# A planner with other durations: longer 1024-element VectorE instructions, longer GpSimd and ScalarE instructions

## Chip, cores and metric

The kernel runs on one core of a Trainium2 chip, in one launch. The metric is the device time of an execution in microseconds. The core has five engines that run side by side, each with its own queue in a fixed order: TensorE (PE; its weight loads are listed apart as PEld), VectorE (DVE), ScalarE (ACT), GpSimd (POOL) and SyncE (SP), which here issues the transfers. An instruction waits on semaphores for what other engines make.

## The reference, cut to what matters

256 tokens of width 1024 in f32 go through two blocks. The first has two layers, each a mixer of four branches and a gated FFN with a short convolution; the second one layer: a two-way state-space scan and attention, then a mixture of experts with 16 experts in four groups, and a last layer norm.

```python
for l in range(DEPTH):                       # DEPTH = 2
    h = rms_norm(x, norm_mix_pre[l])
    proj = h @ w_in[l]                       # queries, keys, values, conv and pool inputs
    ...                                      # o_a: compressed, selected and window attention
    o_b = conformer_conv(b_in, ...)          # depthwise convolution of 31 taps
    o_c = pool_mixer(c_in, ...)
    o_d = banded_attention(qd, ...)          # with sinks
    up = jnp.einsum("bsnc,ncd->bsnd", branches, w_branch[l])
    gates = jax.nn.sigmoid((h @ w_gate[l]).reshape(...))
    mix = jnp.einsum("bsnd,bsnd->bsd", gates, up) @ w_o[l]
    x = x + rms_norm(mix, norm_mix_post[l])
    hf = rms_norm(x, norm_ffn_pre[l])
    u = causal_depthwise_conv(hf @ ffn_w_up[l], ...)
    gate, val = jnp.split(u, 2, axis=-1)
    x = x + rms_norm((gelu(gate) * val) @ ffn_w_down[l], norm_ffn_post[l])
...                                          # second block: scan, attention, MoE, layer norm
```

## The kernel before

**Work.** Nearly all time goes into products of the 256 tokens with weights, 290 MB of f32 that are read from HBM once, mostly in units of 128 x 1024 (512 KB, tiles `wr_wr`). TensorE multiplies a rounded f32 form, so that each unit is split in two: ScalarE copies it into the rounded high half `wh_wh`, and GpSimd or VectorE subtracts this from the unit and writes the low half `wl_wl` (function `sp`). Three products, high x high, low x high and high x low, are then added up in a PSUM bank (`ps_bank`). Activations are split in the same way into `hp_hTh` and `hp_hTl`. Which of the two engines makes a low half is decided while the kernel is written down, by a share for each kind of weight (0.92 of the FFN's go to GpSimd, 0.12 of the experts'), not by the planner.

**Around the products.** VectorE also adds up the 31 taps of the conformer convolution, one instruction for each tap and bank (`ps_bank<-wk_cpad,pp_cwh,ps_bank`), makes softmax rows, their transposed low halves and rotary sums (all `wk_t2k`), the reciprocal square roots of the norms as rows of 128x1 instructions (`wk_sm`, `wk_nw`, `wk_nwy`), normalised tokens (`wk_t4k`, `cp_x`) and the router's numbers (`wk_rt`). ScalarE reads PSUM banks out, takes Squares and exponentials.

**The order.** No instruction is issued when it is written down. The class `Rec` records every one with its engine, its operands and the instructions that it depends on. `Rec.order` then plays a list scheduler (`run`) over the record ten times (`ROUNDS`): each engine takes from its ready instructions the one with the earliest latest-start time, within a small window; PSUM banks and SBUF slots have to be free; transfers have a modelled queue, TensorE a modelled clock. Between VectorE and GpSimd `run` holds a lock: an instruction of one that reads SBUF in the manner marked `port` doesn't start before the last such instruction of the other has ended (`held`). After each round `slack` goes backward through the plan and sets the latest-start times for the next. The shortest of the ten plans is kept, and `emit` issues the instructions in its order, all from one line, which is why every row of the profile carries L540. All durations in this play come from `Rec.cost`, a formula for each engine with a fixed part and a part by elements. They set the order alone: on the chip an instruction starts when its queue and its semaphores allow.

**What the formulas said and what the trace has.** For a split of 128 x 1024, `cost` before gives ScalarE 0.109 + 1024/1200 = 0.962 us, VectorE 0.075 + 1024/920 = 1.188 us, GpSimd 0.148 + 1024/464 = 2.355 us.

## Time and profile before

| | us |
|---|---|
| median of 3 runs | 1503.31 |
| lowest to highest | 1502.95 to 1504.41 |
| the profiled execution | 1503.68 |
| its span | 1501.6 |

The span is the time from the first instruction to the last as the profiler has it; the execution's own time is 2.1 us longer. In the profile, busy time is the time in which an engine executes. A wait is time in which it stood idle before an instruction, put down to the engine and tile whose result came last. The span falls into stages: the first layer's mixer up to about 290 us, its FFN to about 500, the second layer to about 1050, the second block's projections, scan and attention to about 1290, the experts to about 1480, and the last layer norm.

### The profile page before, as it was taken

The page shows a single profiled execution, that of the slowest core. Times are in us where ns is not written, and L with a number is a line of the kernel's source. Part 1 is how long each engine was busy: PE and PEld are TensorE (multiplying, and loading weights), DVE is VectorE, ACT ScalarE, POOL GpSimd, SP SyncE. Part 2 cuts the span into 40 slices and gives each one's busy share as a digit, 9 for nine tenths or more (in the row PEclk, how much of TensorE's full clock was granted, in tenths as well). Part 3 has the DMA queues.
Part 4 walks back from the last instruction along what each step waited for, and adds up shares of the span by engine and source line. Part 5 has one row for each costly group of instructions (what it writes and reads, how often), then busy time and mean ns, then how long its engine had stood idle before and what let it go on. Part 6 is the DMA issues. An engine that isn't in the chain of part 4 may idle for free.

```text
span 1501.6 us, 23962 instructions
## 1 busy us (share of the span) xinstructions
PE 1433.5 (95%) x8276; PEld 1234.6 (82%) x8276; DVE 1035.5 (69%) x2412; ACT 980.7 (65%) x1777; POOL 976.0 (65%) x504
## 2 busy tenths in 40 slices
PE   8989999989999899999999999999999999889994
PEld 6968888879999698788888999999897778768773
DVE  5898622277665779987526733336998876789997
ACT  4876944566555577887447755556677786478772
POOL 5796499848777577947897677776666761342211
PEclk9999999999999999999999999999999999799998
DMA  8555365648888574647757555555543214359881
GB/s 308 167 171 189 114 203 181 215 138 279 281 288 273 188 253 143 207 139 238 240 167 255 162 184 189 186 184 158 169 138 107 94 50 143 127 187 327 332 288 73
DMA packets 91155, 290.35 MB, mean 193 GB/s; under 512 B 11409, under 2 KB 13713, under 8 KB 91026
## 3 DMA queue, kind: packets, MB, share of 16 engines
q1 hardware_dynamic: 91026, 288.74, 57.8%
q8 instruction: 67, 1.10, 0.3%
q14 instruction: 62, 0.51, 0.1%
HBM read 287.13 MB, written 1.05 MB: 192 GB/s over the span
## 4 chain that ended last, share of the span: by engine, by line
PE 82%; DVE 8%; ACT 4%; issue 3%; POOL 1%; DMA 1%; SPq 0%; ACTq 0%; POOLq 0%; DVEq 0%
PE ps_bank L540 82%; DVE ps_bank L540 2%; ACT wh_wh L540 1%; DVE wk_t2k L540 1%; DVE wk_t4k L540 1%; DVE wl_wl L540 1%; POOL wl_wl L540 1%; ACT wk_t2k L540 1%; ACT wk_t4k L540 1%; DVE wk_sm L540 1%; DMA wr_wr<-w_qd 1%; DVE wk_nw L540 0%; ACT hp_hTh L540 0%; ACT ps_bank L540 0%; DVE cp_x L540 0%
## 5 line engine op out<-in xcount | busy, mean ns | idle before, releaser
L540 POOL TENSOR_TENSOR wl_wl<-wr_wr,wh_wh 128x1024 fp32r<-128x1024 f32 (+2 forms) x346 | 822.2, 2386 | 431.2 <-ACT wh_wh L540 416.0
L540 ACT ACTIVATE wh_wh<-wr_wr 128x1024 fp32r<-128x1024 f32 (+2 forms) x446 | 464.0, 1045 | 307.3 <-PE ps_bank L540 185.0
L540 PE MATMUL ps_bank<-hp_hTh,wh_wh 128*128 128x256 f32 x928 | 266.1, 287 | 1.4 <-DVE hp_hTl L540 1.4
L540 PE MATMUL ps_bank<-wh_wh,hp_hTh 128*128 128x512 f32 (+3 forms) x656 | 258.0, 396 | 6.1 <-ACT hp_hTh L540 4.0
L540 PE MATMUL ps_bank<-hp_hTh,wl_wl 128*128 128x256 f32 x928 | 262.8, 283 | 0.2 <-POOL wl_wl L540 0.2
L540 PE MATMUL ps_bank<-hp_hTl,wh_wh 128*128 128x256 f32 x928 | 262.6, 283 | 0.0
L540 PE MATMUL ps_bank<-wl_wl,hp_hTh 128*128 128x512 f32 (+3 forms) x656 | 256.3, 391 | 1.0 <-DVE wl_wl L540 1.0
L540 PE MATMUL ps_bank<-wh_wh,hp_hTl 128*128 128x512 f32 (+3 forms) x656 | 254.8, 389 | 0.6 <-DVE hp_hTl L540 0.6
L540 DVE TENSOR_TENSOR wl_wl<-wr_wr,wh_wh 128x1024 fp32r<-128x1024 f32 (+2 forms) x100 | 152.8, 1543 | 72.3 <-ACT wh_wh L540 70.5
L540 PEld LDWEIGHTS ps_bank<-hp_hTh,wh_wh 128*128 128x128 f32 x928 | 177.6, 191 | 4.3 <-DVE hp_hTl L540 1.7
L540 PEld LDWEIGHTS ps_bank<-hp_hTl,wh_wh 128*128 128x128 f32 x928 | 177.7, 192 | 2.5 <-issue 1.2
L540 PEld LDWEIGHTS ps_bank<-hp_hTh,wl_wl 128*128 128x128 f32 x928 | 177.7, 191 | 0.4 <-POOL wl_wl L540 0.4
L540 PE MATMUL ps_bank<-wh_wh,wk_t4k 128*128 128x512 f32 (+2 forms) x496 | 153.6, 383 | 0.0
L540 PEld LDWEIGHTS ps_bank<-wh_wh,hp_hTh 128*128 128x128 f32 x656 | 124.5, 190 | 33.6 <-ACT hp_hTh L540 6.5
L540 DVE SCALAR_TENSOR_TENSOR wk_t2k<-ps_bank,cl_cols,wk_t2k 128x255 f32<-128x255 f32 (+1 forms) x176 | 84.5, 481 | 96.9 <-ACT wk_t2k L540 94.0
L540 PEld LDWEIGHTS ps_bank<-wl_wl,hp_hTh 128*128 128x128 f32 x656 | 125.2, 191 | 26.9 <-issue 1.9
L540 PEld LDWEIGHTS ps_bank<-wh_wh,hp_hTl 128*128 128x128 f32 x656 | 124.5, 190 | 27.2 <-DVE hp_hTl L540 2.9
L540 DVE SCALAR_TENSOR_TENSOR ps_bank<-wk_cpad,pp_cwh,ps_bank 128x256 f32<-128x256 f32 x232 | 110.2, 486 | 4.4
L540 PEld LDWEIGHTS ps_bank<-wh_wh,wk_t4k 128*128 128x128 f32 x496 | 90.9, 188 | 18.0 <-DVE wk_t4k L540 0.3
L540 ACT ACTIVATE wk_t2k<-ps_bank 128x512 fp32r<-128x512 f32 (+6 forms) x156 | 81.7, 532 | 26.1 <-PE ps_bank L540 23.7
L540 PE MATMUL ps_bank<-wl_wl,wk_t4k 128*128 128x512 f32 (+2 forms) x248 | 94.7, 382 | 0.6 <-DVE wl_wl L540 0.6
L540 ACT ACTIVATE wk_t2k<-wk_t2k,wk_sm 128x128 f32<-128x128 f32 (+2 forms) x200 | 84.8, 457 | 10.0 <-DVE wk_sm L540 9.5
(310 smaller groups left out, 2586.5 us busy)
## 6 DMA issues: line engine op xcount, KB each, us to landing
wr_wr<-w_up SPq DMA_DIRECT2D x88, 512.0 KB, 4.0
wr_wr<-w_gate SPq DMA_DIRECT2D x64, 512.0 KB, 4.2
wm_wm<-w_mod SPq DMA_DIRECT2D x96, 256.0 KB, 4.4
wr_wr<-w_down SPq DMA_DIRECT2D x44, 512.0 KB, 4.3
wr_wr<-w_gu SPq DMA_DIRECT2D x40, 512.0 KB, 5.4
wr_wr<-w_br SPq DMA_DIRECT2D x32, 512.0 KB, 4.5
wk_t4k<-w_gu SPq DMA_DIRECT2D x24, 512.0 KB, 6.6
wr_wr<-w_xbc SPq DMA_DIRECT2D x22, 512.0 KB, 4.4
```

The costliest lines, as they stand in the source:

```text
L540: getattr(getattr(r.nc, o.e), o.f)(*[real(x) for x in o.a], **{n: real(x) for n, x in o.kw.items()})
```

## The change

Three of the durations in `Rec.cost` are set to other values. ScalarE's fixed part grows from 0.066 to 0.08 with a PSUM operand and from 0.109 to 0.13 without, and it takes 1150 instead of 1200 elements a microsecond. GpSimd goes from 0.148 + n/464 to 0.25 + n/440. A VectorE instruction whose largest operand has 1024 elements for each partition, none of them in PSUM, counts 1.55 us. For the 128 x 1024 split that is 1.020 us on ScalarE, 1.55 on VectorE and 2.577 on GpSimd. VectorE's other 1024-element additions and products on SBUF data count 1.55 as well.

```diff
--- before.py
+++ after.py
@@ -255,7 +255,7 @@
         n = max(_size(x) for x in vs)
         ptr = sum(type(o.kw.get(x)) is View for x in ("bias", "scale", "accum_out"))
         if o.e == "scalar":
-            return (0.066 if vs[1].t.psum else 0.109) + n / 1200 + 0.093 * ptr, o.a[2] if len(o.a) > 2 else None
+            return (0.08 if vs[1].t.psum else 0.13) + n / 1150 + 0.093 * ptr, o.a[2] if len(o.a) > 2 else None
         if o.e == "vector":
             if o.f in ("tensor_scalar", "scalar_tensor_tensor"):
                 ptr = sum(type(x) is View and _size(x) == 1 for x in o.a[2:4]) if n > 1 or o.f == "tensor_scalar" else 0
@@ -265,10 +265,12 @@
                 n *= 6
             if o.f in ("tensor_scalar", "tensor_copy", "tensor_single_scalar") and not any(x.t.psum for x in vs):
                 n /= 2
+            if n == 1024 and not any(x.t.psum for x in vs):
+                return 1.55, None
             return 0.075 + n / 920 + 0.06 * ptr, None
         if o.f == "memset":
             return 0.035 + n / 1200, None
-        return 0.148 + n / 464, None
+        return 0.25 + n / 440, None
 
     def follow(r, o, p):
```

The record is the same: the same instructions on the same engines with the same dependencies. The plan made from it differs. 73% of TensorE's instructions keep their place in its queue, 64% of GpSimd's, 47% of ScalarE's and 29% of VectorE's, many of these last being taps of the convolution that exchange places with one another. In the FFN and gate stages the order is nearly the same. Line 540 becomes line 542. The numbers behind the names below count records and differ between the two.

VectorE in the attention of the second layer, before. `wk_sm` is the reciprocal of the softmax sums, the `wk_cpad` rows are taps, and the last two rows make low halves of transposed softmax rows, which TensorE multiplies with the values next:

```order
L540 TENSOR_TENSOR wk_t2k_6441<-wk_t2k_6426,ps_bank_6398 64x512
L540 TENSOR_TENSOR wk_sm_1_6205<-ps_bank_6418,wk_sm_1_6205 128x8
L540 RECIPROCAL wk_sm_6_6455<-wk_sm_1_6205 128x8
L540 SCALAR_TENSOR_TENSOR ps_bank_6109<-wk_cpad_1797,pp_cwh_5545,ps_bank_6109 128x256 x8
L540 TENSOR_TENSOR wk_t2k_6441<-wk_t2k_6489,ps_bank_6453 64x512
L540 SCALAR_TENSOR_TENSOR ps_bank_6109<-wk_cpad_1797,pp_cwh_5545,ps_bank_6109 128x256 x16
L540 TENSOR_TENSOR wk_t2k_6592<-ps_bank_6531,wk_t2k_6582 128x512
L540 TENSOR_TENSOR wk_t2k_6601<-ps_bank_6566,wk_t2k_6587 128x512
```

and after:

```order
L542 TENSOR_TENSOR wk_t2k_6452<-wk_t2k_6425,ps_bank_6395 64x512
L542 TENSOR_TENSOR wk_sm_1_6194<-ps_bank_6412,wk_sm_1_6194 128x8
L542 RECIPROCAL wk_sm_6_6468<-wk_sm_1_6194 128x8
L542 SCALAR_TENSOR_TENSOR ps_bank_6086<-wk_cpad_1810,pp_cwh_5533,ps_bank_6086 128x256 x15
L542 TENSOR_TENSOR wk_t2k_6452<-wk_t2k_6538,ps_bank_6438 64x512
L542 TENSOR_TENSOR wk_t2k_6556<-ps_bank_6518,wk_t2k_6548 128x512
L542 SCALAR_TENSOR_TENSOR ps_bank_6086<-wk_cpad_1810,pp_cwh_5533,ps_bank_6086 128x256 x3
L542 TENSOR_TENSOR wk_t2k_6581<-ps_bank_6554,wk_t2k_6570 128x512
L542 SCALAR_TENSOR_TENSOR ps_bank_6086<-wk_cpad_1810,pp_cwh_5533,ps_bank_6086 128x256
```

The first of the two low halves (128x512, from `ps_bank` and `wk_t2k`), behind 8 and 16 taps before, stands behind 15 taps now, and three taps stand between it and the second.

VectorE ahead of the router, before. `cp_x` is the residual stream, which is normalised here one token tile at a time; BN_AGGR ends the statistics of the second tile:

```order
L540 BN_STATS wk_sm_1_14645<-cp_x_73 128x6
L540 TENSOR_SCALAR cp_x_73<-cp_x_73,wk_sm_14603,wk_nwy_14634 128x512
L540 BN_AGGR wk_sm_14679<-wk_sm_1_14645 128x2
L540 TENSOR_SCALAR wk_nw_14684<-wk_sm_14679 128x1
L540 TENSOR_SCALAR wk_nw_14686<-wk_nw_14684 128x1
L540 TENSOR_SCALAR wk_nw_14691<-wk_nw_14686,wk_nw_14684 128x1
L540 TENSOR_SCALAR wk_nw_14695<-wk_nw_14691 128x1
L540 TENSOR_SCALAR wk_nwy_14697<-wk_nw_14695,wk_nw_14686 128x1
L540 COPY wk_t2k_14699<-ps_bank_14688 128x512
L540 TENSOR_SCALAR wk_nw_14691<-wk_nwy_14697,wk_nw_14684 128x1
```

and after:

```order
L542 BN_STATS wk_sm_1_14648<-cp_x_73 128x6
L542 BN_AGGR wk_sm_14660<-wk_sm_1_14648 128x2
L542 TENSOR_SCALAR wk_nw_14662<-wk_sm_14660 128x1
L542 TENSOR_SCALAR wk_nw_14669<-wk_nw_14662 128x1
L542 TENSOR_SCALAR wk_nw_14672<-wk_nw_14669,wk_nw_14662 128x1
L542 TENSOR_SCALAR wk_nw_14675<-wk_nw_14672 128x1
L542 TENSOR_SCALAR wk_nwy_14677<-wk_nw_14675,wk_nw_14669 128x1
L542 TENSOR_SCALAR wk_nw_14672<-wk_nwy_14677,wk_nw_14662 128x1
L542 TENSOR_SCALAR cp_x_73<-cp_x_73,wk_sm_14617,wk_nwy_14643 128x512
L542 TENSOR_SCALAR wk_nwy_14690<-wk_nw_14672,wk_nwy_14677 128x1
L542 TENSOR_SCALAR wk_sm_14693<-wk_sm_14660,wk_nwy_14690 128x1
L542 TENSOR_SCALAR cp_x_73<-cp_x_73,wk_sm_14660,wk_nwy_14690 128x512
```

The normalisation of the first tile (the first `cp_x<-cp_x,wk_sm,wk_nwy`) stood ahead of the second tile's BN_AGGR and now stands behind it, with six instructions between.

VectorE at the start of the experts, before. The CAST reads a PSUM bank out and the next adds another part:

```order
L540 TENSOR_TENSOR wl_wl_14967<-wr_wr_14562,wh_wh_14959 128x1024
L540 CAST wk_t4k_14976<-ps_bank_14880 128x512
L540 TENSOR_TENSOR wk_t4k_14987<-ps_bank_14880,wk_t4k_14976 128x512
L540 SCALAR_TENSOR_TENSOR wk_t1k_14997<-wk_t1k_14997,ps_bank_14941 128x256
L540 SCALAR_TENSOR_TENSOR wk_t1k_14997<-wk_t1k_14997,wk_ws_14922,ps_bank_14941 128x256
L540 TENSOR_TENSOR wl_wl_15027<-wr_wr_14625,wh_wh_14990 128x1024
L540 TENSOR_TENSOR wl_wl_15048<-wr_wr_14675,wh_wh_15001 128x1024
L540 TENSOR_TENSOR wl_wl_15067<-wr_wr_14649,wh_wh_15013 128x1024
L540 TENSOR_TENSOR wk_t2k_15021<-ps_bank_15017,wk_t2k_15021 128x256
L540 TENSOR_TENSOR wl_wl_15081<-wr_wr_14744,wh_wh_15025 128x1024
L540 TENSOR_TENSOR wl_wl_15085<-wk_t4k_14416,wh_wh_15046 128x1024
L540 SCALAR_TENSOR_TENSOR wk_t1k_15063<-wk_t1k_15063,ps_bank_14994 128x256
```

and after:

```order
L542 TENSOR_TENSOR wl_wl_14966<-wr_wr_14568,wh_wh_14958 128x1024
L542 TENSOR_TENSOR wl_wl_15000<-wr_wr_14601,wh_wh_14977 128x1024
L542 SCALAR_TENSOR_TENSOR wk_t1k_14992<-wk_t1k_14992,ps_bank_14946 128x256
L542 SCALAR_TENSOR_TENSOR wk_t1k_14992<-wk_t1k_14992,wk_ws_14927,ps_bank_14946 128x256
L542 TENSOR_TENSOR wl_wl_15022<-wr_wr_14638,wh_wh_15005 128x1024
L542 TENSOR_TENSOR wl_wl_15050<-wr_wr_14652,wh_wh_14995 128x1024
L542 TENSOR_TENSOR wk_t2k_15037<-ps_bank_15026,wk_t2k_15037 128x256
L542 TENSOR_TENSOR wl_wl_15065<-wr_wr_14715,wh_wh_15020 128x1024
L542 TENSOR_TENSOR wl_wl_15087<-wk_t4k_14416,wh_wh_15031 128x1024
L542 TENSOR_TENSOR wl_wl_15102<-wk_t4k_14465,wh_wh_15062 128x1024
L542 SCALAR_TENSOR_TENSOR wk_t1k_15077<-wk_t1k_15077,ps_bank_14989 128x256
L542 CAST wk_t4k_15052<-ps_bank_14883 128x512
```

The two reads of the bank, second and third before, have gone behind the first splits (the first is the last row here, the second follows two rows later), and the third and the fourth of the `wl_wl` rows have changed places.

## Rows read from the trace of the kernel before

**Rows 1.** The page, span and part 1: busy us, share, instructions.

```profile
span 1501.6 us, 23962 instructions
...
PE 1433.5 (95%) x8276; PEld 1234.6 (82%) x8276; DVE 1035.5 (69%) x2412; ACT 980.7 (65%) x1777; POOL 976.0 (65%) x504
```

**Rows 2.** TensorE's waits: releaser, us in total, times, longest.

```profile
PE ps_bank L540 <- DVE wk_t4k L540: 8.8, 6, 4.2
PE ps_bank L540 <- DVE wl_wl L540: 7.5, 7, 2.2
PE ps_bank L540 <- DVE wk_t2k L540: 4.7, 5, 1.9
...
PE ps_bank L540 <- DVE wk_nw L540: 3.7, 1, 3.7
```

**Rows 3.** The page, part 5: groups with count, busy us, mean ns, idle before.

```profile
L540 POOL TENSOR_TENSOR wl_wl<-wr_wr,wh_wh 128x1024 fp32r<-128x1024 f32 (+2 forms) x346 | 822.2, 2386 | 431.2 <-ACT wh_wh L540 416.0
...
L540 DVE TENSOR_TENSOR wl_wl<-wr_wr,wh_wh 128x1024 fp32r<-128x1024 f32 (+2 forms) x100 | 152.8, 1543 | 72.3 <-ACT wh_wh L540 70.5
...
L540 DVE SCALAR_TENSOR_TENSOR ps_bank<-wk_cpad,pp_cwh,ps_bank 128x256 f32<-128x256 f32 x232 | 110.2, 486 | 4.4
```

**Rows 4.** Timelines, MoE start: start us, duration, instruction, [idle before <-releaser].

```profile
1324.32 0.68 DVE L540 CAST wk_t4k<-ps_bank 128x512 fp32r<-128x512 f32 x1
...
1327.60 9.52 DVE L540 TENSOR_TENSOR wl_wl<-wr_wr,wh_wh 128x1024 fp32r<-128x1024 f32 x3
...
1337.38 3.07 DVE L540 TENSOR_TENSOR wl_wl<-wr_wr,wh_wh 128x1024 fp32r<-128x1024 f32 x1
1340.38 1.21 DVE L540 TENSOR_TENSOR wl_wl<-wk_t4k,wh_wh 128x1024 fp32r<-128x1024 f32 x1
...
1332.70 6.67 POOL L540 TENSOR_TENSOR wk_t4k<-wk_t4k,wk_t4k 128x1024 f32<-128x1024 f32 x2
...
1337.18 0.72 PE L540 MATMUL ps_bank<-wl_wl,wk_t2k 128*128 128x512 f32 x2 [1.88 <-DVE wl_wl L540]
```

**Rows 5.** Timelines and busy time by stretch, second layer's attention.

```profile
585.11 0.50 PE L540 MATMUL ps_bank<-wk_t2k,wk_Vd 128*128 128x512 f32 x1 [1.89 <-DVE wk_t2k L540]
...
584.36 1.29 DVE L540 TENSOR_TENSOR wk_t2k<-ps_bank,wk_t2k 128x512 fp32r<-128x512 f32 x2
...
core 0: us, PE busy (x) PEld busy (x) DVE busy (x) ACT busy (x) POOL busy (x), PEclk, DMA share, GB/s
560.00:630.00 70.00, 65.62 (x375) 54.68 (x374) 65.71 (x172) 58.41 (x130) 60.16 (x37) 1.00 0.54 176
```

**Rows 6.** Timelines of ScalarE and TensorE between the two layers.

```profile
507.06 2.01 ACT L540 ACTIVATE wh_wh<-wr_wr 128x1024 fp32r<-128x1024 f32 x2 [2.26 <-issue]
...
513.25 1.97 PE L540 MATMUL ps_bank<-cp_ident,wk_t4k 128*128 128x128 f32 x8 [4.19 <-DVE wk_t4k L540]
```

**Rows 7.** Timelines of VectorE and TensorE ahead of the router.

```profile
1293.49 1.18 DVE L540 TENSOR_SCALAR cp_x<-cp_x,wk_sm,wk_nwy 128x512 f32<-128x512 f32 x1
...
1305.27 0.18 DVE L540 TENSOR_TENSOR wk_rt<-ps_bank,c_rows 128x20 f32<-128x20 f32 x1 [2.14 <-PE ps_bank L540]
...
1306.49 0.60 PE L540 MATMUL ps_bank<-wk_rt,c_const 128*128 128x8 f32 x2 [1.26 <-DVE wk_rt L540]
```

**Rows 8.** Timelines of TensorE and VectorE near the end of the MoE.

```profile
1468.03 0.50 PE L540 MATMUL ps_bank<-wl_wl,wk_t2k 128*128 128x512 f32 x1 [2.15 <-DVE wl_wl L540]
...
1464.55 3.42 DVE L540 TENSOR_TENSOR wl_wl<-wr_wr,wh_wh 128x1024 fp32r<-128x1024 f32 x1
```

**Rows 9.** Busy time by stretch, columns as in the fifth group.

```profile
512.50:519.50 7.00, 6.07 (x19) 4.47 (x20) 6.82 (x18) 3.96 (x8) 5.98 (x4) 0.56 0.59 199
1338.50:1345.50 7.00, 6.03 (x17) 4.23 (x16) 7.00 (x7) 2.86 (x3) 0.87 (x1) 0.56 0.77 239
1352.00:1482.00 130.00, 123.42 (x539) 97.51 (x538) 125.57 (x139) 93.95 (x113) 24.80 (x9) 1.00 0.78 284
```

## The prediction, made before the changed kernel had run

> **What bounds the kernel now.** The page comes first. TensorE is busy for 1433.5 of 1501.6 us, the other three engines for about two thirds of the span [rows 1]. As the mean share mixes stages, the next view is TensorE's list of waits. Its four lines that matter here hold 24.7 us: VectorE's token sums and normalised rows (`wk_t4k`), the low halves of weights that VectorE makes (`wl_wl`), low halves of softmax rows (`wk_t2k`), and one reciprocal square root (`wk_nw`) [rows 2]. All four end on VectorE. So a new order can gain only where VectorE, or what feeds it, hands TensorE something late; where TensorE runs without a gap (the FFN and gate stages), moving other engines' work about costs and gains nothing as long as it stays ahead.
>
> The change alters no instruction, no dependency and no engine, only the durations from which the planner makes its order. Nothing can be gained by work that is gone. The sum is therefore one of waits: at each place where TensorE waits, I compare what stands ahead of the awaited instruction on its engine before and after, price what moved by its duration in the trace, and ask what is late next.
>
> **What the new durations are worth as numbers.** The VectorE split of 128x1024 takes 1543 ns as a mean over 100, the GpSimd one 2386 ns over 346 [rows 3]. But the VectorE mean is made of two kinds: 1.21 us alone, and about 3.1 us while GpSimd runs an add on SBUF data (three in 9.52 us from 1327.60 on, one of 3.07, one of 1.21; two of GpSimd's adds took 6.67 us together) [rows 4]. The planner already lets one of the two wait for the other (`held` in `run`). With 1.55 for every VectorE instruction of 1024 elements without a PSUM operand it books a part of that price twice, and where there is no GpSimd work it books too much. So the plan isn't simply a truer one; only the places tell.
>
> **The places, one by one.** Gains are positive.
>
> A, attention of the second layer, 571 to 585 us. Before, VectorE ran 24 convolution taps between the reciprocal and the `wk_t2k` subtraction that TensorE waited for; one tap has 486 ns on average over 232 [rows 3]. The subtraction, first of a pair, started at 584.36, and TensorE, idle for 1.89 us, went on at 585.11 [rows 5]. Now 15 taps stand there, and three more come between the pair. That is nine taps or 4.4 us less; four taps ahead of the reciprocal are gone as well. The subtraction's own inputs may hold it up for a part of that, but 1.89 us earlier is within reach, and the wait is gone. What it costs: VectorE may stand still before it, and it is busy for 65.71 of 70 us in this stretch [rows 5], so that the taps put off must still be run. I take 1.5, between 0 (all given back at the next such wait) and 1.9.
>
> B, the norms between the first layer's FFN and the second layer's mixer, 504 to 516 us. ScalarE ran a second weight split ahead of the Squares from which VectorE makes the rstd; two splits took 2.01 us [rows 6], one therefore 1.0. It now stands behind four Squares. TensorE's 4.19 us wait that ended at 513.25 [rows 6] hangs on this chain, but also on VectorE's row of small instructions, of which the Square is only the start. I take 0.7, between 0 and 1.0.
>
> C, layer norm ahead of the MoE router, 1291 to 1306 us. VectorE ran the 1.18 us normalisation of token tile 0 before the statistics of token tile 1 were aggregated; it now comes six small instructions later, and the chain of tile 1 gets ahead of it. The router's first `wk_rt` on tile 1 ran at 1305.27, behind 2.14 us in which VectorE waited for TensorE, and TensorE waited 1.26 us for it in turn [rows 7]. The chain of tile 1 moves up by 1.18 from this alone, and by up to 2 of VectorE's 2.14 us if ScalarE's and TensorE's part of the chain follows. Against that, a weight split of about 1.2 us now stands in front of the copy of tile 0's transposes. I take 1.2, between -0.5 and 2.0.
>
> D, the first weight splits of the MoE, 1324 to 1345 us. Before, VectorE made two reads of a PSUM bank first, from 1324.32 on [rows 4], then met GpSimd's four adds with all of its next four splits: 9.52 us for three, 3.07 for the fourth, and TensorE waited 1.88 us at 1337.18 for one of them [rows 4]. Now the first split comes before the two reads, which move ten places back, and the split that TensorE waited for comes one earlier. The adds' input on ScalarE moves four places back, behind three more splits of 1.0 us each [rows 6]; I estimate that about 2 of these 3 us reach the adds. So about one split less meets an add: one meeting costs 9.52 / 3 - 1.21 = 2.0 us. The reads, however, now fall into the full stretch behind. I take 1.5, between -2 (one meeting more, with the reads in the way) and 3.8 (the 1.88 gone, and as much again of the 7.5 us line [rows 2]).
>
> E, near the end, 1462 to 1470 us. TensorE waited 2.15 us at 1468.03 for a split that took 3.42 us, as it met a GpSimd split that began at the same moment [rows 8]. It now stands three places, some 2.3 us, earlier on VectorE. It may still meet the GpSimd split. I take 1.0, between 0 and 2.15.
>
> F, the norms ahead of the first layer's FFN at 316 us, the wait of 3.7 us for `wk_nw` [rows 2]. Here ScalarE and VectorE run one or two more instructions of the tap's size, half a microsecond each [rows 3], in front of the chain: loss 0.6, between 0 and 1.1.
>
> Elsewhere places of both signs, each under 1 us, are near a wait; I count them at nothing, plus or minus 2.
>
> Sum: 1.5 + 0.7 + 1.2 + 1.5 + 1.0 - 0.6 = 5.3 us. The profiled execution had 1503.68 us, so 1498.4; it lies 0.37 above the median of 1503.31, so the forecast against the median is **1498.0 us**. The half widths of the terms (1.0, 0.5, 1.3, 2.9, 1.1, 0.6 and 2) give about 4 us when they don't all fall to one side: 1494 to 1502 for this case alone.
>
> **A rule against it.** The rows show the meeting itself: while GpSimd adds ran, a VectorE split took 3.2 us and an add 3.3, against 1.21 us for a split alone [rows 4]. The Trainium skill (SBUF — State Buffer, section "Who interferes with whom") says of this that the two share one port pair under an exclusive lock, for the whole instruction, and that the one that comes second blocks. By that rule the price of a split is 1.2 us or that plus the rest of the other's instruction, never 1.55, and the flat figure misleads the planner wherever it has to choose who meets whom; the time by it is the second rival's, 1506.5, instead of 1498. Rows and rule agree on the waiting; which order it makes the planner choose no trace here shows.
>
> **The rivals.**
>
> R1, given back. VectorE's work in the places A, D and E is the same in sum and only exchanged; in the stretch of A it is busy for 65.71 of 70 us and from 1352 to 1482 us for 125.57 of 130, about as much as TensorE with 123.42 [rows 5, 9]. Then a wait removed comes back at the next hand-over, A, D and E are worth nothing, and B, C and F remain: 0.7 + 1.2 - 0.6 = 1.3, which gives 1502.0. For it speak those two lines; against it that TensorE's waits in them sit where VectorE's awaited instruction stood behind work that nobody was waiting for.
>
> R2, more meetings at the port. The four adds of place D and the reads slide into the stretch from 1345 on, where VectorE is full. Each further meeting costs 2.0 us there and nothing hides it. With three more, and nothing gained in D and E, it is 6.0 - (1.5 + 0.7 + 1.2 - 0.6) = 3.2 us slower: 1506.5. It decides from two more meetings on (4.0 - 2.8 = 1.2 slower); with one it is lost in the forecast. For it speaks that the new figures make the planner count a meeting less as something to avoid; against it that GpSimd has just 24.80 us of work in those 130 us [rows 9].
>
> R3, the clock. In the 7 us that follow the long wait at 513 TensorE was granted 0.56 of its clock, mostly the lower of its two levels (1.2 instead of 2.4 GHz), while busy for 6.07 us; after the wait at 1337 it is 0.56 again, with 6.03 us busy [rows 9]. If the waits of B and D shrink so far that the clock doesn't fall behind them, up to 3 us of each are gained: 5.3 + 6 gives 1492. For it speaks that the low stretches begin right after those waits; against it that B leaves 3.5 of 4.19 us standing, and that VectorE paces the other place anyway.
>
> **How the numbers follow.** The forecast gets 0.46, R1 0.26, R2 0.17, R3 0.11. The bound of what a measurement of this kernel tells from no change is 0.2%, 3 us. R3 and nearly all of the forecast lie on the faster side (0.55); R1 and the forecast's upper end are within it (0.28); R2 is slower (0.17). The range has to leave out no more than 2 in 10: it reaches from a part of R3 at 1490 up to half a microsecond beyond R2's 1506.5, as its price per meeting is open.
>
> **What the profile after would show.** TensorE's waits for `wk_t2k` lose the 1.89 us one; the wait between the layers falls from 4.19 to about 3.5; `wk_rt` runs 1 to 2 us earlier against the start of its stage; the splits at the start of the MoE show two or three durations near 3 us instead of four; the wait at 1468 is shorter than 1. Busy times of VectorE and GpSimd change only by meetings: VectorE's 1035.5 us falls by 2 to 4. It is wrong if VectorE's busy time grows by 5 or more (R2), if the waits named are gone but others of their size stand right behind them (R1), or if the granted clock's mean moves by a hundredth (R3, upwards). A new wait in a stage that I took to run without a gap, FFN or gates, would be a cause that none of these holds.

## The result and the profile after

The median after is 1520.76 us over 4 runs (1517.24 to 1525.12), that of before in the same comparison 1503.29. The ratio is 1.0117, with a 95% interval of 1.0102 to 1.0133: the kernel is 17.5 us slower. The forecast was 1498.0 with a range up to 1507, so that sign and range are both wrong. The profiled execution took 1519.78 us, with a mean granted clock of 0.978 (0.981 before).

The page of the kernel after, span and part 1, answers to [rows 1]:

```profile
span 1517.9 us, 23992 instructions
...
PE 1440.6 (95%) x8276; PEld 1237.8 (82%) x8276; DVE 1035.2 (68%) x2412; ACT 981.5 (65%) x1777; POOL 969.9 (64%) x504
```

The counts of the four engines are the same, as they must be. VectorE is busy for 1035.2 us instead of 1035.5, GpSimd for 6.1 us less. TensorE's 8276 instructions took 7.1 us longer, at a mean granted clock that is 0.003 lower; the other 9.2 of the span's 16.3 us are idle time. TensorE's waits in the kernel after (releaser, us in total, times, longest), to be set beside [rows 2]:

```profile
PE ps_bank L542 <- DVE wk_sm L542: 7.3, 5, 3.0
PE ps_bank L542 <- DVE wk_nw L542: 6.4, 2, 6.1
PE ps_bank L542 <- ACT wk_t4k L542: 6.2, 6, 2.6
PE ps_bank L542 <- DVE wk_t4k L542: 5.5, 8, 1.2
PE ps_bank L542 <- DVE wk_t2k L542: 5.4, 7, 1.7
PE ps_bank L542 <- DVE wl_wl L542: 4.9, 5, 2.1
```

Two more lines of before, for the comparison:

```profile
PE ps_bank L540 <- ACT wk_t4k L540: 2.3, 3, 1.4
PE ps_bank L540 <- DVE wk_sm L540: 2.1, 2, 1.3
```

The longest lines of before have shrunk (`wk_t4k` 8.8 to 5.5, `wl_wl` 7.5 to 4.9), as the forecast had it. Others have grown: VectorE's `wk_sm` from 2.1 to 7.3, ScalarE's `wk_t4k` from 2.3 to 6.2, `wk_nw` from 3.7 to 6.4. The groups of low halves in part 5 of the page after, against [rows 3]:

```profile
L542 POOL TENSOR_TENSOR wl_wl<-wr_wr,wh_wh 128x1024 fp32r<-128x1024 f32 (+2 forms) x346 | 818.9, 2376 | 433.6 <-ACT wh_wh L542 399.7
...
L542 DVE TENSOR_TENSOR wl_wl<-wr_wr,wh_wh 128x1024 fp32r<-128x1024 f32 (+2 forms) x100 | 147.9, 1489 | 78.7 <-ACT wh_wh L542 78.3
```

A VectorE split takes 1489 ns on average instead of 1543, so that meetings cost VectorE a little less than before, not more. Yet the idle time before VectorE's splits that ends on ScalarE has grown from 70.5 to 78.3 us.

**Where the time goes.** The engines run the same instructions, so that each TensorE instruction has a twin in before. The table sets the start of an instruction against that of its twin, takes the median over those within 4 us of a stage's edge, and gives what each stage adds (us; plus is lost; stages by the clock of before; one profiled execution of each kernel). E1 has ScalarE's new formula alone, E2 VectorE's, E3 GpSimd's; E8 changes two of ScalarE's numbers by a nanosecond; E17 has 1.55 in the experts alone; E13 is the change with the old formulas in the experts; E20 has other figures. All are told below.

| stage | change | E1 | E2 | E3 | E8 | E17 | E13 | E20 |
|---|---|---|---|---|---|---|---|---|
| 0-285, first mixer | -2.2 | -0.9 | -0.8 | +3.6 | -2.1 | -2.1 | -0.8 | -1.9 |
| 285-340, norms ahead of FFN | +3.3 | +0.1 | +0.4 | +1.9 | +0.4 | 0.0 | +3.1 | +0.7 |
| 340-500, FFN | +0.3 | +0.3 | 0.0 | +0.3 | 0.0 | 0.0 | +0.3 | +0.3 |
| 500-580 | 0.0 | -0.9 | +1.0 | -0.9 | 0.0 | +1.3 | -0.3 | +1.8 |
| 580-600 | -2.3 | -2.0 | -2.5 | -1.4 | -0.6 | +1.6 | -2.3 | -1.5 |
| 600-640, attention | +5.4 | +3.9 | +2.0 | +4.0 | +3.7 | 0.0 | +5.5 | +1.8 |
| 640-785 | +0.1 | -0.5 | +0.9 | -0.8 | -1.1 | +0.5 | +0.1 | +0.4 |
| 785-850, norms ahead of FFN | +4.3 | +3.0 | +2.1 | +10.8 | +2.2 | 0.0 | +4.0 | +2.7 |
| 850-1050, FFN | -0.4 | -0.1 | -0.1 | -0.4 | -0.1 | 0.0 | -0.4 | +0.6 |
| 1050-1235 | +2.8 | 0.0 | -0.8 | -0.4 | -0.6 | 0.0 | +2.8 | +0.6 |
| 1235-1290 | +1.4 | +1.0 | +0.5 | +0.2 | 0.0 | 0.0 | +1.4 | +4.5 |
| 1290-1325, router | -3.0 | -0.5 | +0.2 | -3.5 | -2.9 | +0.1 | -3.0 | +0.2 |
| 1325-1360, first experts | +2.8 | +0.1 | -1.6 | -0.6 | -2.0 | -0.6 | -0.6 | +0.2 |
| 1360-1430, experts | +4.8 | +0.5 | +5.0 | 0.0 | +0.6 | +5.1 | +1.7 | +0.8 |
| 1430-1483, last experts | -1.1 | -2.0 | +1.6 | -1.8 | -1.6 | +2.7 | -1.7 | -1.4 |
| at the end | +16.3 | +1.8 | +7.9 | +10.9 | -4.0 | +8.4 | +9.8 | +9.5 |

E17 also says how far such a table can be trusted: its order is that of before up to the experts, and still its first stage differs by 2.1 us and those around 500 to 600 by 1.3 and 1.6. From 600 to 1325 it keeps to before within 0.1, but for 0.5 in one stage. So the change's -2.2 in the first stage is no gain of its plan: the same order has -2.1 there.

### The profile page after: what moved, and what is told of

Same layout as the page of the kernel before. It is cut to its first block, busy times and chain, and to the rows that moved or that the text cites. A ratio compares the mean times of both kernels' runs of the same rounds, so it can differ in the third digit from the quotient of the medians.

```text
span 1517.9 us, 23992 instructions
## 1 busy us (share of the span) xinstructions
PE 1440.6 (95%) x8276; PEld 1237.8 (82%) x8276; DVE 1035.2 (68%) x2412; ACT 981.5 (65%) x1777; POOL 969.9 (64%) x504
## 4 chain that ended last, share of the span: by engine, by line
PE 66%; DVE 7%; issue 4%; ACT 2%; POOL 1%; DMA 1%; SPq 0%; ACTq 0%; DVEq 0%; POOLq 0%
PE ps_bank L542 66%; DVE ps_bank L542 2%; DVE wl_wl L542 1%; DVE wk_t4k L542 1%; DVE wk_t2k L542 1%; ACT wh_wh L542 1%; DVE wk_sm L542 1%; POOL wl_wl L542 1%; ACT wk_t2k L542 1%; DVE wk_nw L542 0%; ACT wk_t4k L542 0%; ACT ps_bank L542 0%; DMA c_cols<-cols 0%; DMA wr_wr<-w_gu 0%; ACT hp_hTh L542 0%
## 5 line engine op out<-in xcount | busy, mean ns | idle before, releaser
L542 DVE TENSOR_TENSOR wl_wl<-wr_wr,wh_wh 128x1024 fp32r<-128x1024 f32 (+2 forms) x100 | 147.9, 1489 | 78.7 <-ACT wh_wh L542 78.3
```

The lines of the kernel that those rows point to most:

```text
L542: getattr(getattr(r.nc, o.e), o.f)(*[real(x) for x in o.a], **{n: real(x) for n, x in o.kw.items()})
```

## The experiments

First the median in us, then the ratio to the kernel before, both run side by side, with its 95% interval. It is formed over all the executions and can lie 0.1 to 0.2% from the ratio of two medians; costs are added up by it.

**E1 to E4: whose figure.** Each makes one part of the change alone; the fourth adds a nanosecond to VectorE's fixed part, a difference that says nothing about the chip but makes another plan (88% of TensorE's and 46% of VectorE's instructions keep their places). Theory 2 in these expectations is scatter: any new plan of this planner costs about as much.

```diff
 E1  -            return (0.066 if vs[1].t.psum else 0.109) + n / 1200 + 0.093 * ptr, ...
 E1  +            return (0.08 if vs[1].t.psum else 0.13) + n / 1150 + 0.093 * ptr, ...
 E2  +            if n == 1024 and not any(x.t.psum for x in vs):
 E2  +                return 1.55, None
 E3  -        return 0.148 + n / 464, None
 E3  +        return 0.25 + n / 440, None
 E4  -            return 0.075 + n / 920 + 0.06 * ptr, None
 E4  +            return 0.076 + n / 920 + 0.06 * ptr, None
```

> Only ScalarE's new formula; VectorE and GpSimd as before. Theory 1 (the flat 1.55 us for VectorE does the harm, as it books the meetings with GpSimd twice): within 4 us of before, 1500 to 1507. Theory 2 (no single figure does it: any other plan loses some us against the one of before, whose order happens to fit): 1507 to 1518. Theory 3 (GpSimd's 2.577 us does it): as theory 1 here.

> Only VectorE's flat 1.55 us for 1024 elements. Theory 1: nearly the whole loss, 1515 to 1523. Theory 2: a loss of the same kind as in the other three, 1507 to 1518. Theory 3: 1500 to 1507.

> Only GpSimd's new formula. Theory 1: 1500 to 1507. Theory 2: 1507 to 1518. Theory 3: nearly the whole loss, 1515 to 1523.

> None of the three figures: VectorE's fixed part is 0.076 instead of 0.075 us, 1 ns more for each instruction, which says nothing about the hardware but gives another plan. Theories 1 and 3: within 2 us of before. Theory 2: a loss as in the other three runs, 1507 to 1518, since it is the other draw that costs and not the figure.

E1: 1503.59, ratio 0.9998 [0.9985, 1.0012]. E2: 1510.62, 1.0039 [1.0024, 1.0054]. E3: 1513.58, 1.0063 [1.0043, 1.0083]. E4: 1502.28, 0.9982 [0.9967, 0.9997]. The parts cost -0.02 + 0.39 + 0.63 = 1.00%, the whole 1.17 (1.02 to 1.33). ScalarE's figure alone is free, and a new plan alone isn't slower, so theory 2 falls as the sole cause. Theories 1 and 3, each of which put nearly the whole loss (1515 us and more) on one figure, fall too: neither E2 nor E3 gets there.

**E5 to E8: another draw.** If the losses belonged to the particular plans, a nanosecond on top would deal them anew. E5 is the whole change, E6 is E3 and E7 is E2, each with E4's nanosecond; E8 is before with a nanosecond on both of ScalarE's fixed parts. Theory A: the figures cost what they cost, whatever the draw.

```diff
 E5, E6, E7  -            return 0.075 + n / 920 + 0.06 * ptr, None
 E5, E6, E7  +            return 0.076 + n / 920 + 0.06 * ptr, None
 E8          -            return (0.066 if vs[1].t.psum else 0.109) + ...
 E8          +            return (0.067 if vs[1].t.psum else 0.110) + ...
```

> All three figures as in the change, with VectorE's fixed part at 0.076 instead of 0.075 us: another draw of the same kind. Theory A (the figures cost, whatever the draw): 1516 to 1525, like the change. Theory B (each plan is a draw, and the figures only set off another one): 5 us or more away from the change, most likely below it.

> GpSimd's new formula alone, with the same 1 ns on VectorE. Theory A: 1510 to 1517, like the run with GpSimd's formula alone. Theory B, with what the trace of that run shows (ScalarE stands 4.3 us behind a late transfer of a small table at 810 us, 8 us lost in that stretch): 1503 to 1507 if that instruction falls behind others again, 1512 if not.

> VectorE's flat 1.55 us alone, with the same 1 ns on its other instructions. Theory A: 1508 to 1514, and the loss again lies in the experts' stage from 1360 to 1460 us, where VectorE is full. Theory B: 5 us or more away from 1510.6, or the loss lies elsewhere.

> None of the three figures: ScalarE's fixed parts 1 ns longer. Theory A: within 3 us of before. Theory B: spread as wide as between the other kinds, 1500 to 1515.

E5: 1529.47, 1.0141 [1.0096, 1.0186]. E6: 1515.42, 1.0067 [1.0046, 1.0088]. E7: 1518.21, 1.0083 [1.0059, 1.0108]. E8: 1499.96, 0.9971 [0.9954, 0.9989]. The kinds stay apart in sign: in both draws each of the two figures costs 0.4 to 0.8%, and both together about the sum (0.67 + 0.83 = 1.50 in the second, 1.41 measured). But E7 costs twice as much as E2, with intervals that don't touch, and the two null plans gain 0.2 and 0.3%: each plan has several us of its own. Only E6 lies in theory A's range. E5 is 8.7 us above the change and E7 7.6 above E2, both beyond the 5 us that theory B had set; E8 is 4.7 us below the 1504.68 of before beside it, where A gave 3. E7's trace does lose 5.7 us from 1360 to 1430 us, as A had it. So that a figure costs repeats with another draw; how much it costs over the whole kernel doesn't.

**E9 to E12: too long, or merely different?** E9 sets GpSimd's figure as far below the old one as the change sets it above (2.13 us for a split), E10 does that for VectorE (0.83). M1 in these expectations: figures longer than the work do the harm; M2: any distance from the old ones does, on either side; M3: VectorE's 1.55 and the planner's lock count a meeting twice. E11 (with 1.55) and E12 (without) take away the lock, in the plan alone.

```diff
 E9        -        return 0.148 + n / 464, None
 E9        +        return 0.046 + n / 491, None
 E10       +            if n == 1024 and not any(x.t.psum for x in vs):
 E10       +                return 0.83, None
 E11       +            if n == 1024 and not any(x.t.psum for x in vs):
 E11       +                return 1.55, None
 E11, E12  -                        s = max(s0, held) if ops[i].port else s0
 E11, E12  +                        s = s0
```

> GpSimd's formula moved the other way by as much: 0.046 + n/491, 2.13 us for 1024 elements where the change has 2.577 and before 2.355; the trace has 2.39. Theory M1 (a figure that is too long makes the planner issue late what feeds that engine, which the chip's faster engine then waits for; one that is too short doesn't): 1499 to 1507. Theory M2 (distance from the true duration costs, either way): 1509 to 1516, like the long one.

> VectorE's figure for 1024 elements moved the other way by as much: 0.83 us, where the change has 1.55, before 1.188, and a split alone takes 1.21. M1: 1497 to 1506, and VectorE doesn't wait for ScalarE's high halves from 1360 to 1430 us. M2: 1509 to 1518.

> VectorE's flat 1.55 us with the planner's lock between VectorE and GpSimd taken out of the play (on the chip nothing of the lock changes). Theory M3 (the harm is that a meeting is booked twice): as fast as the run with the lock alone taken out, within 3 us. M1: 5 us or more slower than that run, most of it in the experts' stage, where GpSimd has next to nothing to meet with.

> Before, with only the planner's lock taken out of the play: the base for the run with 1.55 us and no lock. The planner then sends VectorE and GpSimd against each other unawares: 1503 to 1515 by every theory; the difference to the other run is what counts.

E9: 1501.19, 0.9982 [0.9973, 0.9992]. E10: 1506.91, 1.0021 [1.0006, 1.0036]. E11: 1511.46, 1.0053 [1.0036, 1.0070]. E12: 1507.05, 1.0018 [1.0005, 1.0032]. A GpSimd figure that is too short costs nothing where one too long by as much costs 0.63%: M2 falls there. VectorE's 0.83 costs 0.21%, half of what 1.55 does; 1506.91 lies between the ranges of M1 and M2, so that M2 isn't excluded for it, though in the experts it loses just 0.3 us. M3 falls in the experts: without the lock 1.55 still loses 4.5 us from 1360 to 1430 us, and the plan with neither gains 1.8. Over the whole kernel 1.55 costs 0.35% without the lock (1.0053 against 1.0018) and 0.39% with it; the 4.4 us between E11 and E12 lie between what M3 (3) and M1 (5) had given.

**E17 and E13: VectorE's figure in the experts.** In the table the experts' stage from 1360 to 1430 us loses with VectorE's figure and only then. E17 puts 1.55 there alone, in the records from 11850 on; E13 is the change without its figures there.

```diff
 E17  +            if o.i >= 11850 and n == 1024 and not any(x.t.psum for x in vs):
 E17  +                return 1.55, None
 E13  +            if o.i >= 11850:
 E13  +                return (0.066 if vs[1].t.psum else 0.109) + n / 1200 + 0.093 * ptr, ...
 E13  -            if n == 1024 and not any(x.t.psum for x in vs):
 E13  +            if o.i < 11850 and n == 1024 and not any(x.t.psum for x in vs):
 E13  -        return 0.25 + n / 440, None
 E13  +        return (0.25 + n / 440 if o.i < 11850 else 0.148 + n / 464), None
```

> Before, with VectorE's flat 1.55 us for the instructions of the experts' stage and of what follows it alone; up to there every engine's order is that of before. Theory M1 (the planner takes VectorE for slower than it is and so lets ScalarE make its high halves late): 1507 to 1511, 4 to 6 us lost from 1360 to 1430 us, and VectorE waits there for ScalarE's high halves, which it didn't before. Rival (that stage only hands on what was lost earlier): within 2 us of before.

> The change, with the three old figures for the instructions of the experts' stage and of what follows it. M1: 5 to 9 us less than the change, 1511 to 1516, and the losses up to 1290 us stay. Rival: within 3 us of the change.

E17: 1511.87 against 1502.88, 1.0058 [1.0041, 1.0075]; 9.0 us slower, and 7.8 of them stand in the table's last two stages. E13: 1513.84, 1.0075 [1.0058, 1.0092], a median 6.9 us below the change's. Busy time by stretch (us, then busy time of PE, PEld, DVE, ACT, POOL with counts, clock, DMA share, GB/s) and VectorE's waits of the same 72 us; first before:

```profile
1358.00:1430.00 72.00, 70.78 (x312) 56.50 (x311) 70.41 (x77) 55.49 (x68) 16.25 (x6) 1.00 0.89 332
```
```profile
DVE ps_bank L540 <- PE ps_bank L540: 0.6, 1, 0.6
DVE wk_t1k L540 <- ACT wk_t1k L540: 0.6, 2, 0.4
```

The same of the kernel after, where the stage comes some 12 us later:

```profile
1370.00:1442.00 72.00, 68.03 (x290) 53.41 (x289) 65.30 (x74) 51.93 (x63) 14.67 (x6) 0.98 0.90 322
```
```profile
DVE wl_wl L542 <- ACT wh_wh L542: 5.8, 8, 1.2
DVE wk_t1k L542 <- ACT wk_t1k L542: 0.3, 1, 0.3
```

Of E17, and at the end VectorE's waits of E13 from 1366 to 1438 us:

```profile
1358.00:1430.00 72.00, 66.93 (x290) 52.05 (x288) 64.50 (x74) 51.50 (x63) 15.00 (x6) 1.00 0.86 321
```
```profile
DVE wl_wl L542 <- ACT wh_wh L542: 4.1, 9, 1.1
DVE wk_t1k L542 <- ACT wk_t1k L542: 3.2, 3, 1.7
```
```profile
DVE wl_wl L544 <- ACT wh_wh L544: 0.8, 2, 0.6
DVE ps_bank L544 <- PE ps_bank L544: 0.8, 1, 0.8
DVE wk_t1k L544 <- ACT wk_t1k L544: 0.4, 1, 0.4
```

Before, VectorE works 70.41 of 72 us here, as much as TensorE, and waits for ScalarE for 0.6. With 1.55 it waits for ScalarE's high halves (`wh_wh`) and copies (`wk_t1k`) for 6.1 and 7.3 us, works 65.3 and 64.5, and the stage is 5 us longer. That holds in all kernels run: in the seven whose experts were planned with 1.55 the stage loses 4.5 to 6.9 us, VectorE waits for ScalarE for 3.1 to 8.0 of 72 us and works 63.2 to 67.2; in the other twelve new ones it loses between -1.8 and 1.7, waits 0.0 to 3.2 and works 68.4 to 71.5. VectorE's work separates the two kinds; the wait alone doesn't (3.1 in E11, which loses 4.5 us, and 3.2 in E20, which loses 0.8).

What the figure does to the order is read from the distances between the engines, medians over VectorE's 41 splits of that stretch; no run tests it. Before, a split starts 0.95 us after ScalarE has ended its high half, and TensorE takes the low half 1.00 us after it is made. After, it is 0.37 and 1.71 us, in E17 0.35 and 1.82, in E13 0.81 and 1.21. In the change and in E17 VectorE thus makes low halves earlier than TensorE needs them and stands close behind ScalarE; as the split really takes 1.21 us alone [rows 4], VectorE can catch up with ScalarE and has to wait. ScalarE's own longest waits there are for TensorE to set a buffer free (`ACT wh_wh <- PE ps_bank`, 8.1 us before, 10.7 after, 16.1 in E17), so that part of the delay may feed itself.

But standing close isn't the cause by itself. E12, with neither 1.55 nor the lock, has 0.38 and 1.52 us and gains 1.8 in the stage; E2 and E14, both with 1.55, have 0.88 and lose 5.0 and 5.6, with VectorE waiting mostly for the copies. What goes with the loss in every kernel is that TensorE stands idle: 4.0 to 5.3 of the 72 us in the seven, 0.0 to 3.0 in the other twelve. TensorE's waits in the same stretches, before, after and in E17:

```profile
PE ps_bank L540 <- ACT wk_t4k L540: 0.7, 1, 0.7
PE ps_bank L540 <- DVE wk_t1k L540: 0.6, 1, 0.6
```
```profile
PE ps_bank L542 <- ACT wk_t4k L542: 2.2, 2, 1.6
PE ps_bank L542 <- POOL wl_wl L542: 1.8, 2, 1.2
```
```profile
PE ps_bank L542 <- ACT wk_t4k L542: 1.6, 1, 1.6
PE ps_bank L542 <- DVE wk_t1k L542: 1.4, 1, 1.4
PE ps_bank L542 <- POOL wl_wl L542: 0.6, 1, 0.6
PE ps_bank L542 <- ACT wk_t2k L542: 0.3, 1, 0.3
```

None of them ends on a low half that VectorE makes. So it is shown that 1.55 in the experts costs this stage 5 us; by which path VectorE's waits become TensorE's is open.

**E14 and E15: two places of GpSimd's figure.** In the norms at 316 us the change put a ScalarE and a VectorE split into the chain that TensorE waits for. E14 is the change with two dependencies, in the plan alone, that keep both splits behind the chain's first instructions. In E3 a table (`c_rows`) is asked for at 805.6 instead of 795.7 us, 6.5 of these 10 us being the lag of the whole kernel by then, and ScalarE stops 4.3 us for it at 814 us. E15 is E3 with a dependency that keeps the waiting instruction (`c_negA`) out of the way.

```diff
 E14  +        for a, b in ((2540, 2490), (2541, 2502)) if len(r.ops) > 8000 else ():
 E14  +            r.follow(r.ops[a], r.ops[b])
 E15  +        if len(r.ops) > 8000:
 E15  +            r.follow(r.ops[6924], r.ops[7034])
```

> The change, with two weight splits ahead of the first layer's FFN (one on ScalarE, one on VectorE) made to wait in the plan for the norm chain that they were placed into. If these two moves cost what the stretch from 285 to 340 us lost: 3 us less there, 1515 to 1519 if nothing else moves. If the chain is late for another reason: TensorE's wait there stays near 6 us. The plan behind it is drawn anew, so the stretch is what counts.

> GpSimd's formula alone, with the small ScalarE instruction that waits for a late table (c_negA) made to stand in the plan behind the read that it followed before. If that one place costs the 8 us of 785 to 815 us: 1504 to 1508. If GpSimd's late splits cost them: 1511 to 1515 as before this edit.

E14: 1520.25, 1.0113 [1.0096, 1.0129]; from 285 to 340 us it loses 2.9 instead of 3.3. The row of TensorE's timeline in E14 at that place:

```profile
320.89 1.08 PE L544 MATMUL ps_bank<-cp_ident,wk_t4k 128*128 128x128 f32 x4 [5.27 <-DVE wk_nw L544]
```

The splits are out of the chain and the wait is still 5.27 us: that theory falls. ScalarE's first Square of the chain and TensorE's last product ahead of the wait, before and in E14:

```profile
307.43 0.60 ACT L540 ACTIVATE wk_t4k<-ps_bank 128x512 f32<-128x512 f32 x1 [4.44 <-PE ps_bank L540]
```
```profile
311.76 0.39 PE L540 MATMUL ps_bank<-wh_wh,hp_hTl 128*128 128x512 f32 x1
```
```profile
312.94 0.60 ACT L544 ACTIVATE wk_t4k<-ps_bank 128x512 f32<-128x512 f32 x1
```
```profile
315.23 0.39 PE L544 MATMUL ps_bank<-wh_wh,hp_hTl 128*128 128x512 f32 x1
```

The Square starts 4.7 us before the end of TensorE's last product in the kernel before, and 2.7 us before it in E14 and in the change, as TensorE took other products ahead of the ones that the chain needs. From the Square to TensorE's next instruction it is 8.5 us before, 8.8 in the change and 8.0 in E14: the chain isn't longer to speak of, it starts later. That is read, not tested. E15: 1511.07, 1.0055 [1.0038, 1.0071]; the median is 2.5 us below E3's, where I had expected 5.6 or more, and by the ratios it is 1.2 us, with intervals that overlap. Rows of E3 at the place, first ScalarE's timeline, then TensorE's:

```profile
814.76 0.23 ACT L540 ACTIVATE c_negA<-c_rows 128x32 f32<-128x32 f32 x1 [4.29 <-DMA c_rows<-rows]
```
```profile
819.18 0.80 PE L540 MATMUL ps_bank<-wh_wh,hp_hTh 128*128 128x512 f32 x1 [5.23 <-DVE cp_x L540]
```

E6, the other draw of E3's figure, has the stop too (3.2 us) and loses 6.8 us from 785 to 815. With ScalarE's stop out of the chain the loss in that stretch falls from E3's 8.2 to 0.8, so that the stop was its cause there. But 2.5 us come back from 815 to 850 (5.1 lost instead of 2.6), and more elsewhere. In the whole change this stop isn't there: it loses 2.2 us from 785 to 815.

**E20 and E19: better figures?** If only figures that are too long do harm (M1), ScalarE's new formula with 1.22 for VectorE (1.21 alone [rows 4]) and 2.40 for GpSimd (2386 ns [rows 3]) should be about as good as before. E19 is E9 with 40 rounds of planning instead of 10.

```diff
 E20  ScalarE as in E1, and
 E20  +            if n == 1024 and not any(x.t.psum for x in vs):
 E20  +                return 1.22, None
 E20  -        return 0.148 + n / 464, None
 E20  +        return 0.148 + n / 455, None
 E19  -ROUNDS = 10
 E19  +ROUNDS = 40
```

> The change's ScalarE formula, with VectorE at 1.22 us for 1024 elements (a split alone has 1.21) and GpSimd at 0.148 + n/455, 2.40 us (the trace has 2.39). M1 (only booking beyond the price alone costs): 1499 to 1507, within 0.25% of before. If the change's loss comes from ScalarE's figure together with any other plan for the rest: 1510 or more.

> Before with GpSimd's figure at 2.13 us as in the run with that figure short, and 40 rounds of planning instead of 10. M1: as that run or a little better, 1496 to 1503. If the gain of that run was chance of its one plan: 1501 to 1508.

E20: 1510.36 against 1503.78, 1.0045 [1.0029, 1.0060], 6.6 us slower, outside what M1 gave and inside what the rival gave (1510 or more: ScalarE's new formula together with any other plan). No run separates the two, since none has E20's other figures with the old formula of ScalarE; E2 and E3 lose without the new one. The experts lose 0.8 us, as M1 has it; the loss sits from 1235 to 1290 us (4.5), 785 to 850 (2.7) and 600 to 640 (1.8), in stages where other plans lose too. E19: 1503.47, 1.0006 [0.9989, 1.0023]; E9's small gain doesn't grow, as the rival (chance of one plan) had it. No kernel run here beats before by more than E8's 0.3%, and E8 differs from before by a nanosecond, so that this is luck, not a recipe.

**What the runs leave.** In the experts VectorE's 1.55 costs 5 us from 1360 to 1430 and 7.2 from 1325 to 1483 (E17); taking the figures away there gives 7.1 back (E13, with all three). With GpSimd's 2.577 all seven kernels lose 1.9 to 3.3 us from 285 to 340 (the other twelve -0.2 to 1.1, but 2.2 in E19) and 4.0 to 5.7 from 600 to 640 (the others -0.4 to 4.9): the first goes with the figure, but for E19; the second may, as E12 loses 4.9 there and E1 and E8 nearly 4 without the figure. Which moved instruction does it is open in both. Most new plans, null ones among them, lose 2 us or more from 785 to 850, where before seems to have had a lucky order. The change's losses from 1050 to 1235 (2.8) and 1325 to 1360 (2.8) appear in neither E2 nor E3 and are open; the second goes with the experts' figures, since E13 is rid of it. So of the change's 17.5 us some 6 to 7 are shown to come from the figures in the experts, and 3 more go with GpSimd's figure ahead of the first FFN. For the rest, about 8 us, no run names the figure; plans that differ by a nanosecond lose some us in the same stages.

## Why the prediction was wrong

**A**, the second layer's attention: right on the spot. The wait of 1.89 us [rows 5] is gone, and 580 to 600 us is 2.3 us shorter (with 1.6 us that the same order can vary there). E1 and E2 gain 2.0 and 2.5 there as well. But from 600 to 640 5.4 us are lost. TensorE's timeline of the kernel after shows waits right behind:

```profile
609.22 0.70 PE L542 MATMUL ps_bank<-wk_t2k,wk_t2k 128*128 128x256 f32 x2 [1.22 <-DVE wk_t4k L542]
...
620.15 0.34 PE L542 MATMUL ps_bank<-cp_ident,wk_t1k 64*128 64x64 f32 x2 [0.98 <-ACT wk_t1k L542]
...
632.81 0.73 PE L542 MATMUL ps_bank<-wh_wh,hp_hTh 128*128 128x512 f32 x2 [1.66 <-DVE wk_t2k L542]
```

That is R1's mechanism, work put off that comes due at the next hand-over, only that more was taken back than given: TensorE is busy 34.01 of these 40 us, at a clock of 0.96. Since E1 with ScalarE's figure alone and E8 with none of the three lose nearly 4 us there, I don't put this down to the figures alone.

**B**, between the layers: worth nothing instead of 0.7. The wait of 4.19 us [rows 6] became two that hold 4.12, and **F**, the norms ahead of the FFN, had the right sign but was mis-sized: 3.3 us instead of 0.6, and the wait grew from 3.7 [rows 2] to 6.13 us. The three rows of TensorE after:

```profile
316.93 2.05 PE L542 MATMUL ps_bank<-cp_ident,wk_t4k 128*128 128x128 f32 x8 [6.13 <-DVE wk_nw L542]
...
513.50 0.66 PE L542 MATMUL ps_bank<-cp_ident,wk_t4k 128*128 128x128 f32 x4 [2.98 <-DVE wk_sm L542]
...
515.30 1.11 PE L542 MATMUL ps_bank<-cp_ident,wk_t4k 128*128 128x128 f32 x4 [1.14 <-DVE wk_t4k L542]
```

F looked at what VectorE and ScalarE run ahead of the chain and named one or two tap-sized instructions; a split of 1.62 us had moved in there. E14 shows that even this wasn't it: as far as the traces tell, I hadn't asked when TensorE itself delivers what the chain starts from.

**C**, the router: gained 3.0 us from 1290 to 1325 where 1.2 was forecast, beyond its upper bound of 2.0. But 1.4 had been lost just before it, and E8, with none of the three figures, gains 2.9 there: the right sign is luck.

**D**, the first experts: the wrong sign, -2.8 instead of +1.5. I had counted on one meeting less. The four adds still met four splits, only later ones: GpSimd's timeline after, then VectorE's, against [rows 4]:

```profile
1334.35 2.40 POOL L542 TENSOR_TENSOR wl_wl<-wr_wr,wh_wh 128x1024 fp32r<-128x1024 f32 x1 [28.62 <-ACT wh_wh L542]
1339.28 2.78 POOL L542 TENSOR_TENSOR wk_t4k<-cp_x,wk_t4k 128x1024 f32<-128x1024 f32 x1 [2.52 <-ACT wk_t4k L542]
1342.56 2.83 POOL L542 TENSOR_TENSOR wk_t4k<-wk_t4k,wk_t4k 128x1024 f32<-128x1024 f32 x1 [0.51 <-ACT wk_t4k L542]
1345.34 3.37 POOL L542 TENSOR_TENSOR wk_t4k<-cp_x,wk_t4k 128x1024 f32<-128x1024 f32 x1
1348.79 3.23 POOL L542 TENSOR_TENSOR wk_t4k<-wk_t4k,wk_t4k 128x1024 f32<-128x1024 f32 x1
```
```profile
1335.61 2.22 DVE L542 TENSOR_TENSOR wl_wl<-wr_wr,wh_wh 128x1024 fp32r<-128x1024 f32 x1 [1.50 <-ACT wh_wh L542]
...
1338.60 4.54 DVE L542 TENSOR_TENSOR wl_wl<-wr_wr,wh_wh 128x1024 fp32r<-128x1024 f32 x2
...
1343.39 3.08 DVE L542 TENSOR_TENSOR wl_wl<-wr_wr,wh_wh 128x1024 fp32r<-128x1024 f32 x1
1346.40 6.71 DVE L542 TENSOR_TENSOR wl_wl<-wk_t4k,wh_wh 128x1024 fp32r<-128x1024 f32 x2
```

The last five splits take 4.54 + 3.08 + 6.71 = 14.3 us; the five of [rows 4] took 13.8. The adds, waiting for ScalarE as I had seen, came later together with the splits that they meet. The rows bear out what I had quoted of the Trainium skill (SBUF — State Buffer, "Who interferes with whom") on the waiting: 3.1 to 3.4 us in a meeting against 1.21 alone. My "never 1.55" was too strong: a split that met only the end of a GpSimd instruction took 2.22 us here, and the one at 312 us 1.62.

**E**, near the end: the 2.15 us wait [rows 8] is gone, and 1430 to 1483 gained 1.1, near the 1.0 taken. But E1, E3 and E8 gain 1.6 to 2.0 there as well, so this is no mark of the change.

**Elsewhere**, counted at nothing plus or minus 2, is the step that failed. The stages of the places A to F gain 2.3 + 0 + 3.0 - 2.8 + 1.1 - 3.3 = 0.3 us together, not 5.3 but no loss. What is lost, 16.6 us, lies elsewhere: the experts (4.8), the stretch behind A (5.4), 785 to 850 us (4.3), 1050 to 1290 (4.3), less 2.2 gained before 285. I had asked where TensorE waited before and whether that wait would shrink. A plan made anew can put waits where none were, and the price of that was readable: in the experts VectorE was busy for 125.57 of 130 us [rows 9] and TensorE for 123.42, so that there was little room for a stop of VectorE. I used those rows for R1 and R2, but not to ask what a figure too long by a quarter does to the order of the engine's feeders. What I had written of the figure ("where there is no GpSimd work it books too much") was the right observation, and these stages have just 16.25 us of GpSimd work in 72; it had no term in the sum. That the FFN stages would not change was right (0.4 us at most).

**The rivals.** R1's mechanism can be read in A, B and D, but it gives back what was gained and can't explain a loss in the experts. R2 had the right sign with the wrong mechanism: VectorE's busy time fell by 0.3 us, where it was to grow by 5. R3 went the other way: the mean clock fell by 0.003, and none of its gain came.

## What to carry to other kernels

In a planner that only sets an order, a figure that is too long on the engine that is full costs time in the stage where it is full: here 4.5 to 6.9 us in seven plans of seven, in a stage of 70 us. A figure that is an average over two kinds of execution (1.21 alone, 3.1 to 3.4 in a meeting) is right for neither; but 1.22, the price alone, didn't make a better plan either (E20). Before forecasting such a change, look not only at the places with waits but at the stages in which two engines have no time to spare: of the 19 new plans seven lost 4.5 us or more in that stage, and only one gained more than 0.1 us (E12, 1.8). And make null plans first: here a nanosecond moved the time by between -0.3% (E8) and +0.4% (E7 against E2), which is the least that any real change of figures must be told from. Over the whole kernel E2's 0.39% and E3's 0.63% are hardly beyond it; what makes the experts' 5 us firm is that they come back in every plan with the figure.

## What was not expected

- The same order can differ by some us in places: E17, ordered as before up to the experts, was 2.2 us ahead at 130 us, lost 1.6 us from 580 to 600, and yet held to within 0.1 us in most stages from 600 to 1325.
- Executions of one kernel differ by several us: those of the kernel after by 7.9 in 4, while the 4 of before beside them lay within 1.5; in the longer comparisons before itself ranged from 1499.8 to 1512.3. So one profile, as in the table, stands for its kernel to a few us: E11's has 1505.14, its other three executions 1511.20 to 1513.33.
- A late 114 KB table stops ScalarE for 4.3 us and costs TensorE 5.2, in a plan whose figures for the transfer hadn't been touched (E3). The change asks for it as late (805.2 us) and has no such stop, as its waiting instruction stands later.
